# A decoder layer with 16384 single-neuron experts: 160 instead of 128 tokens by gathered rows, expert values as matmul weights, 1 MB weight transfers

## The chip, the cores and the metric

The kernel runs on one core of a Trainium2 chip. The core has a matmul engine (TensorE, PE in the profile; its weight loads are listed apart as PEld), three elementwise engines (VectorE = DVE, ScalarE = ACT, GpSimd = POOL), a queue engine (SyncE = SP) and 16 DMA engines between the chip's memory and the on-chip buffer. The metric is the device time of one execution in microseconds (us).

## The reference, cut to what matters

512 tokens of width 2048 pass through one layer: a projection, attention and a recurrent branch, an output projection, and then an expert network (PEER). Only its last part changes:

```python
def chunk(xc):                                   # xc: normalised tokens, (tokens, 2048)
    ...                                          # product keys: 8 heads x top 16 = 128 experts per token
    e = ...                                      # (tokens, 8, 16) expert numbers, of 16384
    g = jax.nn.softmax(top, axis=-1)
    ug = jnp.take(u_tab, e, axis=0)
    act = gelu(jnp.einsum('chkd,cd->chk', ug, xc))
    vg = jnp.take(v_tab, e, axis=0)
    return jnp.einsum('chk,chkd->cd', g * act, vg)
```

Each token picks 128 of 16384 rows of `u_tab` and of `v_tab` (each 16384 x 2048, float32). The result is added to the residual.

## The kernel before, in words

float32 products are made from three matmuls: each operand is split into a part `hi` that the matmul takes exactly and a rest `lo`, and hi·hi, hi·lo and lo·hi are summed (`mm3`, L160; L982 to L984). The splits of weights are L130 (ACT, `hi`) and L131 (DVE, `lo`).

Weights stream through one helper. `order` (L77 to L103) lists units of 128 x 1024 floats (512 KB) in the order of their use; `need` (L135) hands out the next one and calls `emit_next` (L117) for as long as a place is free: it loads a unit (SP's queue, tile `raw`) and splits it. Each pool has two `raw` and two pairs `hi`, `lo`; with an extra pool open there are four of each.

The expert network is done in two ways. The first 128 tokens are **gathered**: for each of a token's 128 experts POOL fetches one row per token, 1 MB at a time (`gather`, L803), and DVE does one operation of 128 x 2048 on it (`side`, L813): for the table u a dot product with the token (L821), for v a multiplication by its weight added to the sum in `acc` (L826). Two tiles take turns for rows. The other 384 tokens (TD) are **dense**: TensorE computes all 16384 experts, and a gate that is zero for all but a token's 128 experts is multiplied on.

- An S job is a block of 128 experts of u: 48 matmuls, `hi`, `lo` of u as weights and 384 tokens as the moving operand (L161 to L163, output `pS`); then Gelu (L959), gate (L904) and split (L913, L916) into `ph`, `pl`. Part of these lie in places of the tiles FH, FL that the gathered tokens no longer need.
- A V job is four blocks times 512 columns of v: 36 matmuls, `ph`, `pl` of 128 tokens as weights and `hi`, `lo` of v, 512 columns, as the moving operand (L982 to L984, output `pV`); DVE adds the three sums to `acc` (L996).

The stages of the expert network, in time: norm and transposition of the tokens (L626 to L640); queries and top-k (the tables' keys, DVE's MAX8 and so on); the gate stage, which makes the gate matrix (L839 to L868) and runs S jobs whose results are stored (`park`, L665; 44 in all); the mixed stage, in which S jobs of the other 84 blocks and V jobs take turns; the tail, V jobs of the 44 stored blocks. In the mixed stage and the tail (`tc.manual_schedule`, L890) every engine works in the order of the code; before, a scheduler sets it. `pace` (L921) calls `side` at a rate: 0.585 per half job, 0.43 in the tail, and some in the gate stage. `post` holds what is to be done with a job's sums; it is emitted in the first half of the next job.

## Time and profile before

| | |
|---|---|
| median of 3 runs | 3100.5 us (3100.32 to 3105.6) |
| the profiled execution: device time | 3107.04 us |
| its span in the profile | 3104.9 us |
| TensorE busy / VectorE busy | 98% / 74% of the span |
| memory traffic | 691 MB, 223 GB/s over the span |
| stages (us from the start) | projections 0 to 297, attention 297 to 580, output projection 580 to 673, norm 673 to 688, top-k 688 to 965, gate 965 to 1349, mixed 1349 to 2700, tail 2700 to 3100 |

A row of matmuls in the profile has a mean duration that is longer than the distance from one to the next, since they are pipelined; what one costs in a stream is read from the starts. In a group's row, what stands behind the bar is idle time of the engine before these instructions and who ended it.

### The profile page before, as it was taken

The page shows a single profiled execution, that of the slowest core. Times are in us where ns is not written, and L with a number is a line of the kernel's source. Part 1 is how long each engine was busy: PE and PEld are TensorE (multiplying, and loading weights), DVE is VectorE, ACT ScalarE, POOL GpSimd, SP SyncE. Part 2 cuts the span into 40 slices and gives each one's busy share as a digit, 9 for nine tenths or more (in the row PEclk, how much of TensorE's full clock was granted, in tenths as well). Part 3 has the DMA queues.
Part 4 walks back from the last instruction along what each step waited for, and adds up shares of the span by engine and source line. Part 5 has one row for each costly group of instructions (what it writes and reads, how often), then busy time and mean ns, then how long its engine had stood idle before and what let it go on. Part 6 is the DMA issues. An engine that isn't in the chain of part 4 may idle for free.

```text
span 3104.9 us, 39324 instructions
## 1 busy us (share of the span) xinstructions
PE 3043.2 (98%) x15443; PEld 2630.8 (85%) x15443; DVE 2284.7 (74%) x3456; ACT 1096.5 (35%) x1371; POOL 393.9 (13%) x280
## 2 busy tenths in 40 slices
PE   8999999999999999999999999999999999999999
PEld 7777565678899998999999999999999999888887
DVE  4465544448999888757777777777777777788887
ACT  4455332342234444443333333333333333333332
POOL 0000000000000011001212112122211212211111
PEclk9999898999999999999999999999999999999999
DMA  7222211232245887678787787877878778878876
GB/s 247 87 78 75 88 55 41 88 108 83 89 129 195 269 274 255 200 264 290 278 296 284 283 301 274 299 284 281 296 281 296 285 282 292 298 277 295 290 283 234
DMA packets 247306, 691.13 MB, mean 223 GB/s; under 512 B 17040, under 2 KB 128272, under 8 KB 213456
## 3 DMA queue, kind: packets, MB, share of 16 engines
q1 hardware_dynamic: 152832, 382.15, 36.8%
q0 software_dynamic: 37008, 269.50, 23.2%
q10 hardware_dynamic: 57280, 36.97, 3.9%
q8 instruction: 121, 1.98, 0.3%
q14 instruction: 65, 0.53, 0.0%
HBM read 650.40 MB, written 38.14 MB: 222 GB/s over the span
## 4 chain that ended last, share of the span: by engine, by line
PE 57%; issue 0%; DVE 0%; ACT 0%
PE pV L984 11%; PE pV L983 11%; PE pV L982 11%; PE pS L161 8%; PE pS L163 8%; PE pS L162 8%; PE ps L161 0%; PE ps L162 0%; PE ps L163 0%; PE ps L863 0%; DVE acc L996 0%; ACT pact L674 0%; DVE o L850 0%; ACT hi L130 0%
## 5 line engine op out<-in xcount | busy, mean ns | idle before, releaser
L130 ACT ACTIVATE hi<-raw 128x1024 fp32r<-128x1024 f32 x631 | 667.8, 1061 | 1489.4 <-PE pS L162 487.6
L131 DVE TENSOR_TENSOR lo<-raw,hi 128x1024 fp32r<-128x1024 f32 x631 | 771.1, 1222 | 495.2 <-ACT hi L130 481.6
L161 PE MATMUL pS<-FH,hi 128*128 128x384 f32 x1344 | 449.9, 335 | 1.3 <-ACT pact L674 1.3
L163 PE MATMUL pS<-FH,lo 128*128 128x384 f32 x1344 | 450.0, 335 | 0.0
L162 PE MATMUL pS<-FL,hi 128*128 128x384 f32 x1344 | 449.5, 334 | 0.0
L984 PE MATMUL pV<-hi,FL 128*128 128x512 f32 x960 | 374.7, 390 | 0.0
L983 PE MATMUL pV<-lo,FH 128*128 128x512 f32 x960 | 374.7, 390 | 0.0
L982 PE MATMUL pV<-hi,FH 128*128 128x512 f32 x960 | 373.4, 389 | 0.0
L161 PE MATMUL ps<-FH,hi 128*128 128x384 f32 (+1 forms) x960 | 342.8, 357 | 0.3 <-ACT hi L130 0.3
L809 POOL DMA_INDIRECT row<-in_un,E x128 | 175.6, 1372 | 1319.3 <-DVE row L821 819.3
L163 PE MATMUL ps<-FH,lo 128*128 128x384 f32 (+1 forms) x960 | 337.8, 352 | 0.6 <-DVE lo L131 0.6
L162 PE MATMUL ps<-FL,hi 128*128 128x384 f32 (+1 forms) x960 | 338.1, 352 | 0.0
L821 DVE SCALAR_TENSOR_TENSOR row<-row,xg 128x2048 f32<-128x2048 f32 x128 | 292.5, 2285 | 22.0 <-DMA row<-in_un,E 22.0
L826 DVE SCALAR_TENSOR_TENSOR acc<-row,W,acc 128x2048 f32<-128x2048 f32 x128 | 300.2, 2345 | 0.0
L809 POOL DMA_INDIRECT row<-in_vn,E x128 | 192.4, 1503 | 804.8 <-DVE acc L826 754.0
L161 PEld LDWEIGHTS pS<-FH,hi 128*128 128x128 f32 x1344 | 252.3, 188 | 4.7 <-ACT pact L674 1.7
L162 PEld LDWEIGHTS pS<-FL,hi 128*128 128x128 f32 x1344 | 252.3, 188 | 3.1
L163 PEld LDWEIGHTS pS<-FH,lo 128*128 128x128 f32 x1344 | 252.2, 188 | 0.0
L996 DVE TENSOR_TENSOR acc<-pV,acc 128x512 f32<-128x512 f32 x384 | 240.9, 682 | 8.3 <-PE pV L984 8.3
L984 PE MATMUL pV<-hi,pl 128*128 128x512 f32 x576 | 224.4, 390 | 0.0
L983 PE MATMUL pV<-lo,ph 128*128 128x512 f32 x576 | 224.2, 389 | 0.0
L982 PE MATMUL pV<-hi,ph 128*128 128x512 f32 x576 | 224.0, 389 | 0.0
(281 smaller groups left out, 4423.2 us busy)
## 6 DMA issues: line engine op xcount, KB each, us to landing
raw<-in_ud SPq DMA_DIRECT2D x256, 512.0 KB
raw<-in_vd SPq DMA_DIRECT2D x256, 512.0 KB
G<-GD SPq DMA_DIRECT2D x33, 768.0 KB
GD<-stg ACTq DMA_DIRECT2D x12, 2048.0 KB
raw<-in_win SPq DMA_DIRECT2D x44, 512.0 KB
raw<-in_wo SPq DMA_DIRECT2D x32, 512.0 KB
raw<-in_wq SPq DMA_DIRECT2D x32, 512.0 KB
AD<-pact ACTq DMA_DIRECT2D x44, 192.0 KB
```

The source lines that it names most:

```text
L130: s.activation(hi, raw, AF.Copy)
L131: v.tensor_tensor(lo, raw, hi.bitcast(F32), op=OP.subtract)
L161: pe.matmul(out, ah, bh, start=start, stop=False)
L162: pe.matmul(out, ah, bl, start=False, stop=False)
L163: pe.matmul(out, al, bh, start=False, stop=stop)
L809: g.indirect_dma_start(out=r, out_offset=None, in_=d["un" if j < 128 else "vn"], in_offset=bass.IndirectOffsetOnAxis(ap=E0[:, j % 128:j % ...
L821: v.scalar_tensor_tensor(r, r, 1.0, xg, op0=OP.mult, op1=OP.mult, accum_out=dots[:, j:j + 1])
L826: v.scalar_tensor_tensor(acc[:, 0, :], r, W0[:, j - 128:j - 127], acc[:, 0, :], op0=OP.mult, op1=OP.add)
L982: pe.matmul(pss[t], ph[:, t, :], hi[:, cs], start=pr + bj == 0, stop=False)
L983: pe.matmul(pss[t], ph[:, t, :], lo[:, cs], start=False, stop=False)
L984: pe.matmul(pss[t], pl[:, t, :], hi[:, cs], start=False, stop=pr + bj == 2)
L996: v.tensor_tensor(a, pss[t], a, op=OP.add)
```

## The change

The gathered tokens become 160: 128 as before (E0) and 32 more (EX). For these 32 the 128 experts are laid out as 4 groups of 32 partitions times 32 columns, so that 32 more gathers of 128 rows serve each table: 320 gathers in place of 256. Rows may live in five homes (a tile A, the place in `acc` of the first 128 tokens, whose residual waits in memory as RD, the tile X of the token operand, and from the mixed stage on Y and C); which row goes where is a list made at build time. The 32 tokens' sums over four groups are added by a matmul with a 0/1 matrix at the end. The dense tokens become TD = 352.

In a V job `hi`, `lo` of v are now the weights (128 columns each) and `ph`, `pl` of 352 tokens the moving operand: 48 matmuls of 352 columns, whose sums are transposed (features by tokens). So `acc` of the dense tokens is transposed once at the start (48 transposes into `hold`, then a copy by POOL into `acc`), and transposed back at the end (`write_out`). The sums of a V job are two tiles of two banks, each added in one DVE operation of 128 x 704. Of eight blocks' `ph`, five lie in FH, FL as 11 pieces of 32 columns, one as 4 pieces of 88, two in tiles of their own.

Weights are loaded 1 MB at a time (two units, 8 KB per partition): `bring` loads into a pool's one `raw` of 128 x 2048, `split` splits a half.

```diff
-TD = S - 128
+TX = 32
+XQ = 128 // TX
+EB = 2
+TG = 128 + TX
+TD = S - TG
...
+    def bring():
+
+        if moved[0] >= len(groups):
+            return False
+        keys, src = groups[moved[0]]
+        ps = pools if moved[1] + len(keys) <= limit[0] else pools[:1]
+        ps = [p for p in ps if not busy[id(p)]]
+        if not ps:
+            return False
+        p = ps[0]
+        moved[0] += 1
+        moved[1] += len(keys)
+        busy[id(p)] = True
+        raw = p.tile([128, 2048], F32, name="raw", bufs=1)[:, :len(keys) * 1024]
+        sy.dma_start(raw, src if len(keys) == 1 else src.rearrange("p u c -> p (u c)"))
+        raws.append([raw, p, len(keys), 0])
+        return True
+
+    def split():
...
         hi = p.tile([128, 1024], F32R, name="hi", bufs=2)
         lo = p.tile([128, 1024], F32R, name="lo", bufs=2)
         s.activation(hi, raw, AF.Copy)
         v.tensor_tensor(lo, raw, hi.bitcast(F32), op=OP.subtract)
...
+        if r[3] == r[2]:
+            raws.pop(0)
+            busy[id(r[1])] = False
         return True
...
-    XH = fbig.tile([128, NTT, KT, 128], F32R, name="FH")
-    XL = fbig.tile([128, NTT, KT, 128], F32R, name="FL")
-    ex = open_extra("ex2", None)
-    fp = pool("ffn")
+    XH = fbig.tile([128, KT, S], F32R, name="FH")
+    XL = fbig.tile([128, KT, S], F32R, name="FL")
+    fp = pool("ffn", side="right")
...
     v.tensor_tensor(xg, xns[0], grow, op=OP.mult)
+    v.tensor_tensor(grow[:TX], xns[1][:TX], grow[:TX], op=OP.mult)
+    sy.dma_start(XD, grow[:TX])
+    sy.dma_start(RD[0:128], acc[:, 0, :])
+    sy.dma_start(RD[128:128 + TX], acc[:TX, 1, :])
+
+    acc2 = acc.rearrange("p t c -> p (t c)")[:, D:D + KT * TD]
+    accT = acc2.rearrange("p (k n) -> p k n", n=TD)
+    hold = fp.tile([128, KT, TD], F32, name="hold")
+    for k in range(KT):
+        ps = bank()
+        for t in range(1, NTT):
+            pe.transpose(ps[:, t * 128:(t + 1) * 128], acc[:, t, k * 128:(k + 1) * 128], ident)
+        s.activation(hold[:, k, :], ps[:, TG:], AF.Copy)
+    g.tensor_copy(acc2, hold.rearrange("p k n -> p (k n)"))
     close(fp)
+    ex = open_extra("ex2", None)
...
+    SLOTS = [(tab, e, j) for tab in ("un", "vn") for e, n in ((E0, 128), (EX, NX)) for j in range(n)]
+    def gather():
+
+        while ng[0] < len(SLOTS):
+            i = ng[0]
+            p = place[i]
+            if not free[p] or p not in home:
+                return
...
+            g.indirect_dma_start(out=r, out_offset=None, in_=d[tab],
+                                 in_offset=bass.IndirectOffsetOnAxis(ap=e[:, j:j + 1], axis=0))
...
-        if q % 3 == 0:
+        if q % 8 in (0, 3, 6):
             park()
-            if q % 6 == 3 or q > 42:
-                side(rowp)
+        if q % 8 == 0 or q % 16 == 11:
+            side()
...
+    def write_out(dc):
+
+        for t0 in range(0, TD, 128):
+            n = min(128, TD - t0)
+            ps = wide()[:, 0]
+            for i in range(4):
+                pe.transpose(ps[:n, i * 128:(i + 1) * 128], accT[:, 4 * dc + i, t0:t0 + n], ident)
+            o = ep.tile([128, NCH, GRP, 32], F32, name="G", bufs=2).rearrange("p c a t -> p (c a t)")[:n, :512]
+            s.activation(o, ps[:n], AF.Copy)
+            s.dma_start(d["out"][TG + t0:TG + t0 + n, dc * 512:(dc + 1) * 512], o)
...
-    RATE = 0.585
+    RATE = 0.81
...
                 for k in range(8):
                     kk = hf * 8 + k
                     mm3(ps, hi[:, k * 128:(k + 1) * 128], lo[:, k * 128:(k + 1) * 128],
-                        XH[:, 1:, kk, :], XL[:, 1:, kk, :], kk == 0, kk == KT - 1)
+                        XH[:, kk, TG:], XL[:, kk, TG:], kk == 0, kk == KT - 1)
...
-                for t in range(3):
+                for i in range(4):
                     for bj in range(2):
                         ph, pl = Pt[gi * GRP + 2 * pr + bj]
-                        cs = slice(bj * 512, (bj + 1) * 512)
-                        pe.matmul(pss[t], ph[:, t, :], hi[:, cs], start=pr + bj == 0, stop=False)
-                        pe.matmul(pss[t], ph[:, t, :], lo[:, cs], start=False, stop=False)
-                        pe.matmul(pss[t], pl[:, t, :], hi[:, cs], start=False, stop=pr + bj == 2)
+                        ws = slice(bj * 512 + i * 128, bj * 512 + (i + 1) * 128)
+                        pe.matmul(pss[i], hi[:, ws], ph, start=pr + bj == 0, stop=False)
+                        pe.matmul(pss[i], lo[:, ws], ph, start=False, stop=False)
+                        pe.matmul(pss[i], hi[:, ws], pl, start=False, stop=pr + bj == 2)
...
-                pace(0.43 if tail else RATE)
+                pace(0.4 if tail else RATE)
...
+                for i, pw in enumerate(pws):
+                    a = accT[:, 4 * dc + EB * i:4 * dc + EB * (i + 1), :]
+                    v.tensor_tensor(a, pw[:, :, :TD], a, op=OP.add)
```

What it moves is seen in the order of each engine's instructions. First TensorE, from a V job to an S job in the mixed stage, before (pV and pS are sums, behind the arrow stand both operands, FH and FL here are blocks' `ph`, `pl` or the tokens; the last numbers are the output's partitions x columns):

```order
L982 MATMUL pV<-hi,FH 128x512
L983 MATMUL pV<-lo,FH 128x512
L984 MATMUL pV<-hi,FL 128x512
L161 MATMUL pS<-FH,hi 128x384
L162 MATMUL pS<-FL,hi 128x384
L163 MATMUL pS<-FH,lo 128x384
```

The same place now:

```order
L1129 MATMUL pw<-FH,hi 128x352
L1130 MATMUL pw<-FH,lo 128x352
L1131 MATMUL pw<-FL,hi 128x352
L191 MATMUL pw<-FH,hi 128x352
L192 MATMUL pw<-FL,hi 128x352
L193 MATMUL pw<-FH,lo 128x352
```

Both kinds of job are now 48 matmuls of 352 columns. Second ScalarE at the end of the norm stage, before (FH is the `hi` of the tokens, `hi<-raw` the split of weights, qT the first query's copy):

```order
L630 ACTIVATE xn_4165<-acc,r_4153 128x2048
L130 ACTIVATE hi<-raw 128x1024
L637 ACTIVATE FH<-ps,vec 128x4x128 x16
L130 ACTIVATE hi<-raw 128x1024 x3
L730 ACTIVATE qT<-ps 128x512
```

The same place now:

```order
L671 ACTIVATE xn_4097<-acc,r_4085 128x2048
L677 ACTIVATE FH<-ps,vec 128x512 x16
L693 ACTIVATE hold<-ps 128x352 x16
L152 ACTIVATE hi<-raw 128x1024 x2
L784 ACTIVATE qT<-ps 128x512
```

The 16 copies into `hold` stand before the next split of weights, and that split goes into tiles that lie where `hold` lay, so it also waits for POOL's copy out of `hold` (L694). Third SP's queue in the mixed stage, before (`raw` from u and v, G the gates of four blocks):

```order
L127 DMA raw<-in_ud 128x1024 x2
L127 DMA raw<-in_vd 128x1024
L895 DMA G<-GD 128x12x128
L127 DMA raw<-in_vd 128x1024
L127 DMA raw<-in_ud 128x1024 x2
```

The same place now:

```order
L135 DMA raw<-in_vd 128x2048
L135 DMA raw<-in_ud 128x2048
L1025 DMA G<-GD 128x11x128
L135 DMA raw<-in_vd 128x2048
L135 DMA raw<-in_ud 128x2048
```

Two loads of 512 KB have become one of 1 MB, of which two places exist in place of four of half the size.

## Rows read from the trace of the kernel before

**Rows 1.** The page: span, and busy time of TensorE and VectorE.

```profile
span 3104.9 us, 39324 instructions
PE 3043.2 (98%) x15443; PEld 2630.8 (85%) x15443; DVE 2284.7 (74%) x3456; ACT 1096.5 (35%) x1371; POOL 393.9 (13%) x280
```

**Rows 2.** Busy time by stretch: norm, top-k, gate, mixed, tail; columns in the first line.

```profile
core 0: us, PE busy (x) PEld busy (x) DVE busy (x) ACT busy (x) POOL busy (x), PEclk, DMA share, GB/s
...
688.00:965.00 277.00, 276.15 (x1401) 245.23 (x1402) 257.51 (x947) 88.72 (x117) 0.00 (x0) 1.00 0.34 108
965.00:1349.00 384.00, 359.49 (x2769) 351.17 (x2768) 299.84 (x600) 174.42 (x196) 31.81 (x26) 0.97 0.75 243
...
1700.00:2200.00 500.00, 500.00 (x2542) 456.64 (x2542) 386.52 (x400) 155.24 (x182) 101.87 (x71) 1.00 0.81 290
...
2700.00:3095.00 395.00, 395.00 (x1744) 327.06 (x1743) 338.62 (x371) 121.64 (x141) 66.27 (x41) 1.00 0.80 281
```

**Rows 3.** TensorE in order of time, three starts (us): V half job, S job, V job.

```profile
1893.08 0.39 PE L982 MATMUL pV<-hi,ph 128*128 128x512 f32 x1
...
1897.16 0.33 PE L161 MATMUL pS<-FH,hi 128*128 128x384 f32 x1
...
1905.50 0.39 PE L982 MATMUL pV<-hi,FH 128*128 128x512 f32 x1
```

**Rows 4.** TensorE in order of time: matmuls of 128 columns with own weights.

```profile
704.35 0.94 PE L691 MATMUL ps<-keys,qT 128*128 128x128 f32 x7
```

**Rows 5.** VectorE in order of time, mixed stage.

```profile
1895.51 2.29 DVE L821 SCALAR_TENSOR_TENSOR row<-row,xg 128x2048 f32<-128x2048 f32 x1
1897.72 0.08 DVE L821 DVE_READ_ACCUMULATOR row<-row,xg 128x1 f32 x1
1898.45 1.23 DVE L131 TENSOR_TENSOR lo<-raw,hi 128x1024 fp32r<-128x1024 f32 x1 [0.64 <-ACT hi L130]
1899.59 1.88 DVE L996 TENSOR_TENSOR acc<-pV,acc 128x512 f32<-128x512 f32 x3
...
1907.77 0.55 DVE L904 TENSOR_TENSOR pact<-pact,G 128x384 f32<-128x384 f32 x1
1908.91 0.56 DVE L916 TENSOR_TENSOR FL<-pact,FH 128x384 fp32r<-128x384 f32 x1 [0.59 <-ACT FH L913]
```

**Rows 6.** Groups of VectorE, 1700 to 2200 us: count, busy us, mean ns, idle before.

```profile
L131 DVE TENSOR_TENSOR lo<-raw,hi 128x1024 fp32r<-128x1024 f32 x121 | 148.0, 1223 | 92.6 <-ACT hi L130 92.6
```

**Rows 7.** DMA queues, 1700 to 2200 us: packets, MB, time of 16 engines; a gather's landing.

```profile
q1 hardware_dynamic: 29772, 69.46, 41.0%
q0 software_dynamic: 10290, 74.99, 39.2%
...
row<-in_un,E POOLq DMA_INDIRECT x54, 7.2
```

**Rows 8.** Two stretches of 10 us with the DMA engines full (columns as in Rows 2).

```profile
2040.00:2050.00 10.00, 10.00 (x51) 8.95 (x50) 7.63 (x10) 2.65 (x3) 2.29 (x2) 1.00 0.99 370
2580.00:2590.00 10.00, 10.00 (x51) 8.95 (x50) 6.41 (x6) 3.87 (x5) 0.94 (x1) 1.00 1.05 388
```

**Rows 9.** Groups by shape: weight split; POOL's sum; gate; ScalarE's copy; VectorE's scaling.

```profile
L130 ACT ACTIVATE hi<-raw 128x1024 fp32r<-128x1024 f32 x631 | 667.8, 1061 | 1489.4 <-PE pS L162 487.6 <-PE ps L162 402.1 <-PE pV L984 362.5
...
L332 POOL TENSOR_TENSOR xs<-xs,yg 128x512 f32<-128x512 f32 x4 | 5.2, 1298 | 81.7 <-ACT yg L331 81.5
...
L863 PE MATMUL ps<-o,o 128*128 128x128 bf16 x1152 | 75.8, 223 | 24.5 <-ACT stg L865 12.3 <-DVE o L850 11.4
L959 ACT ACTIVATE pact<-pS 128x384 f32<-128x384 f32 x84 | 39.7, 473 | 0.0
...
L628 DVE TENSOR_SCALAR xn<-acc,r 128x2048 f32<-128x2048 f32 x2 | 2.5, 1284 | 0.0
```

**Rows 10.** The end, in order of time; and landing of a 1 MB output (us).

```profile
3099.82 0.69 DVE L996 TENSOR_TENSOR acc<-pV,acc 128x512 f32<-128x512 f32 x1 [0.67 <-PE pV L984]
3100.55 0.38 ACTq L999 DMA_DIRECT2D out<-acc  x1
...
out<-acc POOLq DMA_DIRECT2D x1, 1024.0 KB, 4.4
```

**Rows 11.** Projections of 512 columns, moving operand in one piece (XH) and in four (FH).

```profile
L161 PE MATMUL ps<-XH,hi 128*128 128x512 f32 x352 | 142.2, 405 | 7.8 <-ACT hi L130 7.8
...
L161 PE MATMUL ps<-FH,hi 128*128 128x512 f32 x256 | 101.0, 395 | 0.0
```

More of the change, by code (lines that the diff above doesn't have):

```diff
@@ L154, in close_extra @@
         pools.remove(p)
-        assert all(r[2] is not p for r in ready.values())
+        assert all(r[2] is not p for r in ready.values()) and all(r[1] is not p for r in raws)
         if last[0] is p:
@@ L791, in body @@
         park()
+        if t == 1:
+            ei = tk.tile([128, 128], I32, name="ei")
+            v.scalar_tensor_tensor(ei[:TX], ef[0][:TX], 128.0, ef[1][:TX], op0=OP.mult, op1=OP.add)
+            sy.dma_start(ED, ei[:TX])
+            sy.dma_start(HD, gf[:TX])
+            for q in range(XQ):
+                rows_, cols_ = slice(q * TX, (q + 1) * TX), slice(q * 128 // XQ, (q + 1) * 128 // XQ)
+                sy.dma_start(EX[rows_], ED[:, cols_])
+                sy.dma_start(GX[rows_], HD[:, cols_])
         if t > 1:
@@ L801, in body @@
     rows, ng = {}, [0, 0]
-    def gather(*pools):
-        j = ng[0]
-        if j >= 256:
-            return
-        ng[0] += 1
-        r = pools[j % len(pools)].tile([128, D], F32, name="row", bufs=1)
-        g.indirect_dma_start(out=r, out_offset=None, in_=d["un" if j < 128 else "vn"],
-                             in_offset=bass.IndirectOffsetOnAxis(ap=E0[:, j % 128:j % 128 + 1], axis=0))
-        rows[j] = r
-    def side(*pools):
-        j = ng[1]
-        if j >= 256:
+    NX = 128 // XQ
@@ new lines, in body @@
+    SLOTS = [(tab, e, j) for tab in ("un", "vn") for e, n in ((E0, 128), (EX, NX)) for j in range(n)]
+    U1, V0, V1 = 128, 128 + NX, 256 + NX
+    NG0 = NCH + NCH // 2 + 1
+    home, used_at, place, late = {"A": rowp.tile([128, D], F32, name="rowA"), "B": acc[:, 0, :], "X": xg}, {}, [], {}
+    for i in range(len(SLOTS)):
+        if i < NG0:
+            c = "AB"
+        elif i < U1:
+            c = "ABCY" if i < U1 - 4 else "ABC"
+        elif i < V0:
+            c = "ABCX" if i < V0 - 4 else "ACX"
+        elif i < V1:
+            c = "ACXY" if i < V1 - 4 else "ACY"
+        else:
+            c = "ACY"
+        if i in (U1, V0):
+            used_at["X" if i == U1 else "Y"] = i + 0.5
+        p = min(c, key=lambda p: used_at.get(p, -1))
+        used_at[p] = i
+        place.append(p)
@@ new lines, in body @@
+    free = {p: True for p in "ABCXY"}
+    last_use = {p: {} for p in "ABCXY"}
+    ycut, bcut = max(i for i in range(U1) if place[i] == "Y"), max(i for i in range(V0) if place[i] == "B")
+    xcut = max(i for i in range(V1) if place[i] == "X")
+    def gather():
[4 more added lines that the diff above has]
+                return
+            ng[0] += 1
+            free[p] = False
+            tab, e, j = SLOTS[i]
+            r = home[p]
+            g.indirect_dma_start(out=r, out_offset=None, in_=d[tab],
+                                 in_offset=bass.IndirectOffsetOnAxis(ap=e[:, j:j + 1], axis=0))
+            rows[i] = r
@@ L829, in side @@
-        gather(*pools)
+        for p in freed:
+            free[p] = True
+        freed.clear()
+        r = rows.pop(i)
+        tab, e, j = SLOTS[i]
+        first, n = e is E0, 128 if e is E0 else NX
+        if tab == "un":
+            x_ = xg if first else home["Y"]
+            v.scalar_tensor_tensor(r, r, 1.0, x_, op0=OP.mult, op1=OP.mult, accum_out=dots[:, j:j + 1])
+            if j == n - 1:
+                w, g_ = (W0, G0) if first else (WX, GX)
+                s.activation(w, dots[:, :n], AF.Gelu)
+                v.tensor_tensor(w, w, g_, op=OP.mult)
+        elif first:
+            v.scalar_tensor_tensor(acc[:, 0, :], r, W0[:, j:j + 1], acc[:, 0, :], op0=OP.mult, op1=OP.add)
+            if j == n - 1:
+                g.dma_start(d["out"][0:128, :], acc[:, 0, :])
+        elif j == 0:
+            v.tensor_scalar(xg, r, WX[:, 0:1], None, op0=OP.mult)
+        else:
+            v.scalar_tensor_tensor(xg, r, WX[:, j:j + 1], xg, op0=OP.mult, op1=OP.add)
@@ L831, in body @@
+        freed.append(place[i])
+        if i == ycut:
+            freed.pop()
+            for q in range(XQ):
+                g.dma_start(home["Y"][q * TX:(q + 1) * TX], XD)
+        elif i == bcut:
+            freed.pop()
+            g.dma_start(acc[:, 0, :], RD[0:128])
+        elif i == xcut:
+            freed.pop()
+        if i == U1 - 1:
+            freed.append("X")
+        elif i == V0 - 1:
+            freed.append("Y")
+        gather()
     gp = pool("gate")
@@ L924, in pace @@
             debt[0] -= 1
-            side(rowp, ep)
-    gather(rowp, ep)
+            side()
+    gather()
     post = []
```

177 lines of the change are left out of this document (101 added, 76 removed).

## The prediction, made before the changed kernel ran

> **What bounds the kernel now.** I read the page's busy times first, then the same by stretch, then starts in order of time, since a matmul's duration in a group's row overlaps with its neighbours'. The page puts TensorE at 98% of the span and VectorE at 74% [rows 1]. By stretch [rows 2] TensorE is busy 500.00 of 500 us in the mixed stage, 395.00 of 395 in the tail and 276.15 of 277 in top-k; only the gate stage leaves it 24.5 us. The granted clock is 1.00 in the mixed stage and the tail, the upper of its two levels. So a matmul that becomes shorter shortens these stages, until something else does not keep up. The candidates stand in the same row of the mixed stage: VectorE 386.5 of 500, and the DMA engines at a share of 0.81, moving 290 GB/s.
>
> **What a matmul costs.** Between 1893.08 and 1897.16 lie 18 matmuls of 512 columns, so 226.7 ns each; between 1897.16 and 1905.50 lie 48 of 384 columns, 173.8 ns each [rows 3]. The difference is 0.413 ns a column, which leaves a fixed 15.0 ns, and 352 columns come to 160.5 ns. That is below anything shown with float32 operands of this kind, so I ask whether loading the weights becomes the bound: seven matmuls of 128 columns, each with weights of its own of the same size, took 0.94 us, at most 134 ns each [rows 4]. That is less than 160.5, so the line holds.
>
> **The terms, against the profiled execution's 3107.0 us** (it stands 6.5 us above the median of 3100.5; the sum is a difference, and I take it off the median).
>
> S jobs: 48 matmuls, 8.34 us before, 7.70 now, 128 of them: −81 us. V jobs: 36 × 226.7 ns = 8.16 us before, 48 × 160.5 = 7.70 now, 128 of them: −59. There are more matmuls than before and yet it is less, since 4 × 352 columns replace 3 × 512; the twelve extra fixed costs are in the 160.5. Gate matrix: 88 steps in place of 96; a step's matmuls keep TensorE busy 75.8/96 = 0.79 us [rows 9]: −6. Together −146.
>
> Norm stage: 48 transposes at up to 0.134 us are 6.4 us, and the 16 copies into `hold` at 0.47 us (L959's, of 384 columns) 7.6, of which TensorE, eight banks ahead, sees about 6. What stands behind them is a chain: POOL's copy of 128 x 5632, then the split of the next query weights (1.06 and 1.22 us) [rows 6, 9]. TensorE has one load, 48 × 227 ns = 10.9 us, in hand meanwhile. POOL's copy is not in the trace. At the pace of its sum of two operands, 1298 ns for 512, it takes 14.3 us, and TensorE waits about 9; at that of VectorE's scaling of one operand, 1284 ns for 2048, 3.5 us, and the chain is hidden. I take a copy of 7 us and a wait of 2, half of the nearest row on POOL itself, since one operand is read in place of two. The term is +8, bounds 6 and 15. The Trainium skill (GPSIMD Engine Reference, section Engine selection) says that operations with one input run on GpSimd roughly at VectorE's line rate; by that the wait of 2 us goes. No run so far shows it.
>
> End: the last sum was added at 3099.82, the span ended 5.1 us later [rows 10]. Now the last two column groups leave by six copies through two tiles, so three rounds of a copy (0.5 us) and a write, at most the 4.4 us of a 1 MB write [rows 10], and the 32 tokens' sum runs beside that: 9 to 15 us in place of 5, I take +6. Transposing back the two column groups before it puts 24 transposes into the tail and makes TensorE wait for VectorE's addition a job early: +6. Together +12, bounds 8 and 18.
>
> Loads of 1 MB: in projections and top-k an extra pool is open and 10.9 us of matmuls cover a load. In the attention stage only one place is left, and a unit can be loaded only when the one before it has been split: half of the gather's 7.2 us for 1 MB [rows 7] plus 2.3 us of split is 5.9 us against 24 × 227 ns = 5.4 us of matmuls, for ten units: +5 with nothing between them, 0 if attention's own matmuls lie between, and below 0 nothing, as TensorE was not waiting for loads there. I take +3.
>
> Mixed stage, 80 pairs of an S and a V job, 16.5 us each before and 15.4 by TensorE alone. The cost of 64 more gathers lies here, since `pace` now asks for 0.81 per half job: 3.24 rows a pair in place of 2.34. VectorE, by distances between starts [rows 5]: four `lo` at 1.14, the sums 1.88, gate and split 1.70 with the wait for ScalarE, 2.34 rows at 2.21: 13.3 us of 16.5. Now two additions of 704 columns at 0.80 (0.60 for 512, and 1.05 ns a column from `lo` against it), so 4.56 + 1.60 + 1.70 + 7.16 = 15.0 us of 15.4. It was idle 92.6 us in 500 waiting for `hi` [rows 6], that is, ahead of TensorE; this cushion goes. Behind a late VectorE wait the sums: before, they were added by 1901.47, 4.3 us after the V job's end [rows 5], and a bank came round again two V jobs later; now the second tile is needed when the next V job starts, 7.7 us on.
>
> DMA: a pair moved 2 × 1.05 + 2.34 × 1.05 + 0.2 MB (gates) = 4.75 MB in 16.5 us, the 290 GB/s of rows 2. Now it is 2.10 + 3.40 + 0.18 = 5.68 MB in 15.4 us, 369 GB/s. The engines' time per MB is 16 × 500 × 0.410/69.46 = 47 us on q1 (pieces of 4 KB) and 42 us on q0 (8 KB) [rows 7]; with weights in pieces of 8 KB too, 5.68 MB take 238 us of 16 engines, 14.9 us of 15.4. So three resources are at 97% and over. What speaks for holding 369 is that whole stretches of 10 us ran at 370 and 388 [rows 8], and that a row has four homes, so some 15 us from issue to use in place of 12. Bounds: 0, if TensorE stays at 500 of 500; and at the far end the 290 GB/s of now, 19.6 us a pair, +336. I take the rate nearest to rows 8, a little under 370: 360 GB/s, 15.75 us a pair, 80 × 0.35 = +28. The Trainium skill (DMA: Bandwidth & Descriptors, section Specifications) gives about 358 GB/s as the memory's limit for one core; by it a pair takes 15.9 us and the term is +37. Both stretches of rows 8 are above that limit, so the trace does not agree with it for short times.
>
> Tail: a V job moves 1.05 + 0.84 + 0.36 MB in 7.7 us, 292 GB/s against 281 [rows 2], and VectorE has 0.8 rows in place of 0.86: nothing changes there. GpSimd's more gathers and the EX lists cost nothing as long as VectorE is what they wait for.
>
> Sum: −146 + 8 + 12 + 3 + 28 = −95, so 3012 by the profiled execution and 3006 by the median.
>
> **Rivals.** (1) TensorE stays the only bound: +0 in the mixed stage, +0 for loads and the low ends elsewhere: −146 + 14 = −132, 2968 us. For it: 500 of 500 now. Against: the three shares above. (2) The mixed stage goes over to DMA or VectorE: 16.2 to 16.9 us a pair (351 to 336 GB/s), +64 to +120, 3042 to 3098. For it: the share of 0.81 at 290 GB/s, scaled to 369, is 1.03. Against: larger pieces cost less, and rows 8. (3) Slower: the DMA engines cannot hold 335 GB/s over the whole stage. Everything but the mixed stage is worth −123, or 1.54 us a pair; 5.68 MB in 16.9 us are 335 GB/s, and below that the change loses. At 320 GB/s a pair takes 17.75 us, 3166 us in all. For it: no stretch of 500 us has shown more than 290. Against: those were not asked for more, since TensorE never waited. (4) Moving operands in 11 pieces of 32 columns, five of eight blocks, 3840 matmuls: if a piece had a price of 2.2 ns, 25 ns a matmul, it would eat the gain of 95; at the fixed 15 ns each it would be +580. Against: 512 columns in one piece and in four have means of 405 and 395 ns [rows 11], so a piece costs nothing that shows.
>
> **Chances.** Forecast (2985 to 3030) 0.55; rival 1 0.20; rival 2 0.17; rival 3 0.05; rival 4 0.03. The range of 8 in 10 goes from just under rival 1 to the middle of rival 2: 2960 to 3065. A measurement of this kernel can tell about 0.2%, 6 us, from no change. Faster by more than that: 0.90; within it 0.03; slower 0.07.
>
> **What would show it.** S and V jobs both at 7.7 us apart in the tail, matmuls 160 ns apart: rival 4 is out. In the mixed stage TensorE's idle time and who ended it: VectorE's `lo` or sums (late VectorE), or `hi` behind a load (late DMA); GB/s of the stretch near 360. A wait of TensorE for `hi` just after the first query weights shows POOL's copy, whose row then has its duration. Wrong would be: TensorE idle in the tail, top-k longer by more than 15 us, or matmuls of 352 columns no faster than those of 384.

## The result, and the profile after

The changed kernel takes 3029.9 us (median of 4 runs, 3025.2 to 3040.8); the kernel before, on the same chip, 3103.05 (3100.3 to 3113.5). The ratio is 0.9763, 95% interval 0.9727 to 0.9799: 73 us faster. The forecast was 3006 with a range of 2960 to 3065. The profiled execution took 3028.0 us, its span is 3026.0 us. The page (busy time of each engine, share, instructions), against [rows 1]:

```profile
span 3026.0 us, 41804 instructions
...
PE 2932.1 (97%) x16987; PEld 2692.1 (89%) x16987; DVE 2370.1 (78%) x3391; ACT 1082.9 (36%) x1392; POOL 576.2 (19%) x350
```

Busy time by stretch, for top-k, gate, mixed stage and tail, against [rows 2]:

```profile
core 0: us, PE busy (x) PEld busy (x) DVE busy (x) ACT busy (x) POOL busy (x), PEclk, DMA share, GB/s
699.00:990.00 291.00, 281.71 (x1436) 248.79 (x1435) 262.27 (x955) 90.16 (x120) 11.23 (x5) 0.98 0.34 122
990.00:1356.00 366.00, 328.21 (x2640) 319.00 (x2639) 260.27 (x531) 162.99 (x185) 16.32 (x13) 0.95 0.64 212
1700.00:2200.00 500.00, 499.21 (x3088) 498.91 (x3087) 461.41 (x439) 161.43 (x195) 176.08 (x109) 1.00 0.96 369
2625.00:3010.00 385.00, 381.39 (x2345) 380.24 (x2344) 324.80 (x324) 122.06 (x145) 62.14 (x39) 1.00 0.77 281
```

In the mixed stage TensorE is as busy as before, while VectorE went from 386.5 to 461.4 of 500 us, and the DMA engines from a share of 0.81 and 290 GB/s to 0.96 and 369. In the gate stage TensorE is idle for 38 of 366 us and its granted clock is 0.95: that stretch became worse.

Where the time went, by the first matmul of each stage, the tail from the end of the last S job (the forecast's terms are put on stages by the number of jobs: 11, 33 and 84 S jobs in top-k, gate and mixed stage; 80 and 48 V jobs in mixed stage and tail):

| stage | before | after | difference | forecast |
|---|---|---|---|---|
| projections | 297.4 | 305.9 | +8.5 | 0 |
| attention, output projection | 380.2 | 374.5 | -5.7 | +3 |
| norm to first query weights | 10.2 | 18.5 | +8.3 | +8 |
| top-k | 282.8 | 291.2 | +8.5 | -7 |
| gate | 380.2 | 366.5 | -13.7 | -27 |
| mixed | 1349.1 | 1266.3 | -82.7 | -63 |
| tail | 399.9 | 390.4 | -9.5 | -16 |
| after the last V matmul | 5.2 | 12.6 | +7.4 | +6 |
| span | 3104.9 | 3026.0 | -78.9 | -95 |

A V job, an S job and the next V job in the mixed stage, TensorE in order of time, against [rows 3]:

```profile
1891.75 0.32 PE L1129 MATMUL pw<-FH,hi 128*128 128x352 f32 x1
...
1899.64 0.32 PE L191 MATMUL pw<-FH,hi 128*128 128x352 f32 x1
...
1907.31 0.32 PE L1129 MATMUL pw<-FH,hi 128*128 128x352 f32 x1
```

The S job takes 7.67 us, 159.8 ns a matmul; the V job 7.89 us, 164.4 ns. VectorE's groups (count, busy, mean ns, idle before) and the DMA engines in 1700 to 2200 us, against [rows 6, 7]:

```profile
L153 DVE TENSOR_TENSOR lo<-raw,hi 128x1024 fp32r<-128x1024 f32 x129 | 157.0, 1221 | 18.8 <-ACT hi L152 18.7
L1143 DVE TENSOR_TENSOR acc<-pw,acc 128x704 f32<-128x704 f32 x66 | 55.5, 882 | 0.0
```

```profile
DMA packets 35953, 184.52 MB, mean 369 GB/s; under 512 B 2895, under 2 KB 14159, under 8 KB 14159
## 3 DMA queue, kind: packets, MB, share of 16 engines
q0 software_dynamic: 15309, 111.15, 56.4%
q1 hardware_dynamic: 20610, 72.89, 38.8%
```

VectorE's cushion, the time it waits for `hi`, fell from 92.6 to 18.8 us, as forecast, but nothing came through it to TensorE. The gate matrix, against the row of L863 in [rows 9], where 24.5 us of idle time stood:

```profile
L989 PE MATMUL ps<-o,o 128*128 128x128 bf16 x1056 | 73.4, 224 | 42.2 <-DVE o L976 40.7
```

The longest of these waits, ScalarE, VectorE and TensorE in order of time:

```profile
1024.74 0.38 ACTq L994 DMA_DIRECT2D GD<-stg  x1
...
1046.74 2.73 ACT L991 ACTIVATE stg<-ps 128x512 f32<-128x512 f32 x3 [14.86 <-DMA GD<-stg]
1049.28 1.99 ACT L152 ACTIVATE hi<-raw 128x1024 fp32r<-128x1024 f32 x2
1050.36 1.23 DVE L153 TENSOR_TENSOR lo<-raw,hi 128x1024 fp32r<-128x1024 f32 x1 [10.78 <-ACT hi L152]
...
1054.52 0.29 PE L989 MATMUL ps<-o,o 128*128 128x128 bf16 x1 [12.97 <-DVE o L976]
```

Read from the bottom: TensorE waits 13 us for one-hot products, VectorE is late with them since it stood 10.8 us before a `lo`, whose `hi` stands on ScalarE behind a copy into `stg`; and `stg`, of which there is one, was still being written to memory, 22 us after that write was issued.

The norm stage (VectorE and GpSimd in order of time):

```profile
682.61 2.29 DVE L680 TENSOR_TENSOR xg<-xn,grow 128x2048 f32<-128x2048 f32 x1 [1.76 <-DMA grow<-in_fg]
684.94 2.28 DVE L681 TENSOR_TENSOR grow<-xn,grow 32x2048 f32<-32x2048 f32 x1
687.15 10.61 DVE L678 SCALAR_TENSOR_TENSOR FL<-ps,vec,FH 128x512 fp32r<-128x512 f32 x16
...
700.18 4.89 POOL L694 COPY acc<-hold 128x5632 f32<-128x5632 f32 x1 [108.71 <-ACT hold L693]
...
706.24 2.35 DVE L153 TENSOR_TENSOR lo<-raw,hi 128x1024 fp32r<-128x1024 f32 x2
```

The start (SyncE's loads, then TensorE) and the end (VectorE, ScalarE, SyncE), in order of time:

```profile
1.68 0.42 SPq L135 DMA_DIRECT2D raw<-in_win  x1
...
2.62 0.43 SPq L230 DMA_DIRECT2D cst<-in_cst  x1
7.12 0.33 SPq L221 DMA_DIRECT2D xs<-in_xT  x1
7.49 2.85 SPq L135 DMA_DIRECT2D raw<-in_win  x2
...
19.81 0.79 PE L191 MATMUL ps<-XH,hi 128*128 128x512 f32 x1 [2.85 <-ACT XH L225]
...
3013.50 0.89 DVE L1143 TENSOR_TENSOR acc<-pw,acc 128x704 f32<-128x704 f32 x1 [1.03 <-PE pw L1131]
3016.67 0.59 ACT L1077 ACTIVATE G<-pw 96x512 f32<-96x512 f32 x1 [1.07 <-DMA out<-G]
...
3022.02 0.34 SPq L1163 DMA_DIRECT2D out<-rowA  x1
```

### The profile page after: what moved, and what is told of

Its sections match the earlier page's. It is cut to its first block, busy times and chain, and to the rows that moved or that the text cites. A ratio compares the mean times of both kernels' runs of the same rounds, so it can differ in the third digit from the quotient of the medians.

```text
span 3026.0 us, 41804 instructions
## 1 busy us (share of the span) xinstructions
PE 2932.1 (97%) x16987; PEld 2692.1 (89%) x16987; DVE 2370.1 (78%) x3391; ACT 1082.9 (36%) x1392; POOL 576.2 (19%) x350
## 4 chain that ended last, share of the span: by engine, by line
PE 67%; DVE 10%; issue 8%; DMA 8%; POOL 4%; ACT 3%; ACTq 0%; POOLq 0%; SPq 0%; DVEq 0%
PE pw L1129 8%; PE pw L1131 8%; PE pw L1130 7%; PE ps L191 6%; PE ps L193 6%; PE ps L192 6%; PE pw L191 5%; PE pw L193 4%; PE pw L192 4%; DMA GD<-stg 3%; DVE lo L153 3%; PE ps L421 2%; PE ps L422 2%; PE ps L423 2%; DVE acc L934 2%
## 5 line engine op out<-in xcount | busy, mean ns | idle before, releaser
L1129 PE MATMUL pw<-FH,hi 128*128 128x352 f32 x1536 | 502.0, 327 | 4.5 <-DVE acc L1143 3.3
L1131 PE MATMUL pw<-FL,hi 128*128 128x352 f32 x1536 | 501.9, 327 | 0.0
L1130 PE MATMUL pw<-FH,lo 128*128 128x352 f32 x1536 | 500.0, 326 | 0.0
L191 PE MATMUL pw<-FH,hi 128*128 128x352 f32 x1344 | 434.3, 323 | 0.6 <-ACT pact L728 0.6
L193 PE MATMUL pw<-FH,lo 128*128 128x352 f32 x1344 | 433.9, 323 | 0.0
L192 PE MATMUL pw<-FL,hi 128*128 128x352 f32 x1344 | 433.2, 322 | 0.0
L193 PE MATMUL ps<-FH,lo 128*128 128x352 f32 (+1 forms) x960 | 332.1, 346 | 4.9 <-DVE lo L153 4.9
L191 PE MATMUL ps<-FH,hi 128*128 128x352 f32 (+1 forms) x960 | 336.6, 351 | 0.0
L192 PE MATMUL ps<-FL,hi 128*128 128x352 f32 (+1 forms) x960 | 331.8, 346 | 0.0
L1129 PEld LDWEIGHTS pw<-FH,hi 128*128 128x128 f32 x1536 | 288.8, 188 | 6.0 <-issue 4.1
L1131 PEld LDWEIGHTS pw<-FL,hi 128*128 128x128 f32 x1536 | 288.9, 188 | 0.0
L1130 PEld LDWEIGHTS pw<-FH,lo 128*128 128x128 f32 x1536 | 288.7, 188 | 0.0
L191 PEld LDWEIGHTS pw<-FH,hi 128*128 128x128 f32 x1344 | 252.9, 188 | 0.9 <-ACT pact L728 0.9
L192 PEld LDWEIGHTS pw<-FL,hi 128*128 128x128 f32 x1344 | 253.4, 189 | 0.0
L193 PEld LDWEIGHTS pw<-FH,lo 128*128 128x128 f32 x1344 | 252.4, 188 | 0.0
L1143 DVE TENSOR_TENSOR acc<-pw,acc 128x704 f32<-128x704 f32 x256 | 215.5, 883 | 8.4 <-PE pw L1131 8.3
L191 PEld LDWEIGHTS ps<-FH,hi 128*128 128x128 f32 x960 | 184.4, 192 | 14.4 <-issue 4.4
## 6 DMA issues: line engine op xcount, KB each, us to landing
GD<-stg ACTq DMA_DIRECT2D x11, 2048.0 KB, 12.2
```

The lines of the kernel that those rows point to most:

```text
L191: pe.matmul(out, ah, bh, start=start, stop=False)
L192: pe.matmul(out, ah, bl, start=False, stop=False)
L193: pe.matmul(out, al, bh, start=False, stop=stop)
L1129: pe.matmul(pss[i], hi[:, ws], ph, start=pr + bj == 0, stop=False)
L1130: pe.matmul(pss[i], lo[:, ws], ph, start=False, stop=False)
L1131: pe.matmul(pss[i], hi[:, ws], pl, start=False, stop=pr + bj == 2)
```

## The experiments

e1 to e8 and e11 are edits of the changed kernel, e9 is one of e8, e10 and e12 of e9. The kernel before had medians of 3105 to 3110 us beside them, so runs are compared by their ratio to it; the changed kernel's is 0.9763 (0.9727 to 0.9799).

| run | median us | ratio to before, 95% | norm starts | top-k | gate | mixed | tail | end |
|---|---|---|---|---|---|---|---|---|
| changed kernel | 3029.9 | 0.9763 | 680.5 | 291.2 | 366.5 | 1266.3 | 390.4 | 12.6 |
| e1 gate rows | 3007.9 | 0.9670 (0.9654, 0.9686) | 682.9 | 289.1 | 345.5 | 1281.9 | 391.8 | 12.5 |
| e2 start | 3034.1 | 0.9747 (0.9726, 0.9769) | 679.7 | 290.8 | 373.2 | 1269.2 | 389.9 | 12.5 |
| e3 pieces | 3021.8 | 0.9727 (0.9705, 0.9750) | 679.9 | 287.8 | 367.5 | 1264.4 | 389.8 | 12.6 |
| e4 extra load | 3108.6 | 0.9991 (0.9979, 1.0004) | 680.8 | 288.9 | 372.5 | 1337.3 | 401.1 | 12.5 |
| e5 other place | 3017.0 | 0.9716 (0.9690, 0.9741) | 669.3 | 287.5 | 363.3 | 1266.7 | 389.5 | 12.6 |
| e6 roles alone | 3186.2 | 1.0259 (1.0233, 1.0285) | 675.2 | 285.8 | 390.1 | 1379.5 | 421.3 | 14.0 |
| e7 half MB | 3026.5 | 0.9740 (0.9718, 0.9763) | 671.5 | 288.3 | 360.3 | 1280.9 | 386.7 | 12.2 |
| e8 together | 3008.0 | 0.9681 (0.9658, 0.9703) | 674.0 | 287.6 | 348.9 | 1274.9 | 397.9 | 9.8 |
| e9 sum last | 2997.3 | 0.9650 (0.9635, 0.9665) | 673.7 | 290.0 | 346.8 | 1264.5 | 390.1 | 11.8 |
| e10 rows slower | 3007.7 | 0.9679 (0.9666, 0.9693) | 671.7 | 287.9 | 348.0 | 1263.5 | 404.6 | 11.8 |
| e11 one bank | 3029.2 | 0.9751 (0.9736, 0.9766) | 677.4 | 287.9 | 372.3 | 1265.6 | 391.9 | 12.1 |
| e12 rows later | 3004.5 | 0.9669 (0.9652, 0.9686) | 673.5 | 291.4 | 340.7 | 1272.5 | 387.7 | 11.8 |

The stages are those of each profiled execution. The mixed stage of one kernel can differ by some 15 us between executions (e1's profiled one, at 3024.1, is its slowest of five). Stages that an edit did not touch differ too: top-k takes 287.5 to 291.2 us in the eleven kernels whose top-k is that of the changed kernel, the gate stage 360.3 to 373.2 in the seven that have its gate stage and its tokens. One execution cannot tell smaller differences than these.

**The roles alone** (e6): the 32 tokens are dense again.

```diff
-TG = 128 + TX
+TG = 128
...
-    RATE = 0.81
+    RATE = 0.59
...
```

> The 32 extra tokens are dense again: 384 dense tokens, 256 gathers in four homes (A, B, C, X) at 0.59 per half job, all else as in the changed kernel (values as weights, sums two banks at a time, 1 MB loads). Theory A (the gain is the 32 tokens' alone, and changing the roles of the V matmuls by itself costs): S jobs 8.34 us as before, V jobs 48 x about 175 ns = 8.4 us against 8.16 before, +31 us; norm stage +8, end +6, projections +8: 3145-3165 with the kernel before at 3105. Rival B (the roles, the larger sums or the 1 MB loads bring a share of the 73 us themselves): 3060-3105.

Measured: 3186 us, slower than before by 2.6%. Theory A holds, with a larger price than its 3145 to 3165. An S job, a V job and the next S job:

```profile
1893.45 0.34 PE L191 MATMUL pw<-FH,hi 128*128 128x384 f32 x1
...
1901.89 0.34 PE L1098 MATMUL pw<-FH,hi 128*128 128x384 f32 x1
...
1910.29 0.34 PE L191 MATMUL pw<-FH,hi 128*128 128x384 f32 x1
```

The S job takes 8.44 us (8.34 before), the V job 8.40 and on average 48 x 176.8 ns = 8.49, against 8.16 in the old arrangement. So the new roles lose 0.3 us a job; they are what lets 32 tokens fewer shorten the V matmul at all, and these 32 are worth about 155 us (1.0259 - 0.9763 of 3105).

**The gate stage** (e1).

```diff
-    GD = dr.tile([NCH, NBLK // GRP, 128, GRP * 32], F32, name="GD")
+    GD = dr.tile([NCH, 128, NBLK // GRP, GRP * 32], F32, name="GD")
...
-            s.dma_start(GD[q // 8].rearrange("g p x -> p g x"), stg[0].rearrange("p (g a) t -> p g (a t)", a=GRP))
+            s.dma_start(GD[q // 8], stg[0].rearrange("p (g a) t -> p g (a t)", a=GRP))
...
```

> The stored gate matrix GD is laid out so that a partition's 16 KB are written in one piece (before: 32 pieces of 512 B); nothing else changes. Theory A (the gate stage lost its gain because ScalarE waits in order for the 2 MB write of stg, with the weight splits queued behind it): ScalarE's wait for GD, 68.1 us in the gate stage, falls below 30, TensorE's and its loads' wait for the one-hot products, 58.9 us, falls below 25, the gate stage goes from 366.5 to 330-345 us, the run to 2998-3010. Rival B (VectorE works the gathered rows in order between the one-hots, and that is what delays them): the GD wait falls, TensorE's wait stays above 45, the run stays at 3024-3036. Rival C (the write is slow from the traffic beside it, not from its pieces): the write still lands after 11 us or more and nothing changes.

Measured: 3007.9 us, gate stage 345.5, just above the 330 to 345 of theory A. ScalarE's wait for GD fell from 68.1 to 36.6 us, less than expected; the first write is free after 13.6 us instead of 22.0. TensorE's row, and ScalarE's wait (us in total, times, longest):

```profile
L989 PE MATMUL ps<-o,o 128*128 128x128 bf16 x1056 | 71.7, 224 | 23.4 <-DVE o L976 22.5
```

```profile
ACT stg L991 <- DMA GD<-stg: 36.6, 10, 6.6
```

Theory A holds: the order of rows on VectorE was not touched, and TensorE's idle time went from 42.2 to 23.4 us, about the 24.5 of the kernel before.

**The start** (e2, e5).

```diff
-        if m == 0:
+        if m < 2:
...
```

> The weights of the second input block, like those of the first, are loaded as two transfers of 512 KB; all else 1 MB as in the changed kernel. Theory A (projections lost 8.5 us because 1 MB of later weights goes ahead of the token loads that TensorE needs): TensorE's waits for XH and hi behind the first matmul, 5.9 us, fall below 2, attention starts at 298-301 us instead of 305.9, the run is 4-8 us faster than the changed kernel. Rival B (the 1 MB loads cost time through the whole stage, by the single place per pool): attention starts at 304-306, the run changes by less than 2 us.

Measured: attention starts at 305.1, and the wait of 2.85 us for XH is still there at 19.85. Theory A falls in this form. SyncE's rows after show why: the second `raw` is issued at 7.49, since its place is that of the first, which has to be split before. The choice of place was next:

```diff
-        p = ps[0]
+        p = min(ps, key=lambda p: when.get(id(p), 0))
+        when[id(p)] = moved[0] + 1
...
```

> A load goes to the pool whose place was used longest ago, instead of to the first that is free (in the changed kernel the second half of the first input block waits for the place of the first half to be split and is issued at 7.49 us, beside the third token load, instead of at 2.60). Theory A (the 1 MB place costs the start, since two loads in a row use one place and token loads stand behind them): TensorE's waits for XH and XL in the first 36 us, 4.7 us, go below 1.5, attention starts at 297.5-301 us instead of 305.9, the run is 5-8 us faster than the changed kernel. Rival B (the 8.5 us come from the clock or from traffic that stays): attention starts at 304-306, change below 2 us.

Measured: attention starts at 297.4, as before the change, the waits for XH and XL are 0.7 us, and the run is 3017.0. Theory A holds for the waits. For the whole run its gain is not shown: the interval of its ratio overlaps that of the changed kernel. The second load now leaves at once (SyncE in order of time):

```profile
1.68 0.42 SPq L136 DMA_DIRECT2D raw<-in_win  x1
2.14 0.43 SPq L223 DMA_DIRECT2D xs<-in_xT  x1
2.62 0.43 SPq L136 DMA_DIRECT2D raw<-in_win  x1
```

Not all of the 8.5 us is the place, though. Four later kernels with this choice (e8, e9, e10, e12) start attention at 299.4 to 301.8 us, the changed kernel and the other runs that load 1 MB into the first free place at 301.7 to 308.5. TensorE's granted clock differs with it: in the first 36 us it was 1.00 before the change, in e5 and in e10, 0.95 in e8, e9 and e12, and 0.91 in the changed kernel. So the choice of place takes the waits away each time, and of the 8.5 us 4.1 to 6.5 came back in the later kernels.

**The pieces of the moving operand** (e3).

```diff
-        if q < 5:
-            ph, pl = XH[:, 0:NCH, 32 * q:32 * q + 32], XL[:, 0:NCH, 32 * q:32 * q + 32]
+        if q < 4:
+            av = a.rearrange("p (c t) -> p c t", c=4)
+            ph, pl = (X[:, 4 * q:4 * q + 4, 0:TD // 4] for X in (XH, XL))
...
```

> Of eight blocks' ph, pl, four lie in 4 pieces of 88 columns and two in 8 pieces of 44 (changed kernel: five in 11 pieces of 32, one in 4); two in tiles of their own as before. In the changed kernel matmuls with 11 pieces start 164.3 ns apart on average, with 4 pieces 161.3, with one 160.3. Theory A (a piece costs about 0.4 ns): those with 8 pieces come to about 163, the mean over V jobs from 163.1 to about 161.5, mixed stage and tail together 8-11 us shorter. Rival B (the place, not the pieces: operands in FH, FL are slower than in tiles of their own): all in FH, FL stay at 163-165, change below 3 us.

An S job, a V job (all operands in 4 pieces) and the next S job:

```profile
1895.54 0.32 PE L191 MATMUL pw<-FH,hi 128*128 128x352 f32 x1
...
1903.26 0.33 PE L1130 MATMUL pw<-FH,hi 128*128 128x352 f32 x1
...
1910.95 0.32 PE L191 MATMUL pw<-FH,hi 128*128 128x352 f32 x1
```

The V job takes 7.69 us, 160.2 ns a matmul, in FH and FL all the same: rival B falls. But theory A's price per piece is wrong too: operands in 8 pieces have a median distance of 163 to 164 ns, like those in 11; those in 4 have 160, like one. Mixed stage and tail of the profiled executions differ by only 2.5 us, because TensorE waited 9.3 us in V jobs there instead of 4.5. The medians differ by 8 us, but the intervals of the two ratios overlap: the shorter distance between matmuls is shown, a gain of the whole run is not.

**The limit of the DMA engines** (e4).

```diff
+    def extra():
+        sy.dma_start(XT[nx[0] % 2], d["un"][128 * (nx[0] % 100):128 * (nx[0] % 100) + 128, 0:256])
+        nx[0] += 1
...
+                extra()
...
+                if not tail:
+                    extra()
...
```

> In each half job of the mixed stage 128 KB more are loaded (pieces of 1 KB) into a tile that nothing reads: 403 GB/s would be asked for instead of 369. Theory A (DMA still has room above 369, TensorE alone bounds the stage): mixed stage 1266 us plus at most 10, run 3025-3040. Rival B (369 to 385 GB/s is what the DMA engines can do, the stage stands right at their limit): at 385 GB/s a pair takes 16.1 us instead of 15.4, mixed stage +40 to +60; at 370 GB/s 16.8 us, +110; TensorE then waits for hi and lo. Run 3070-3140.

Measured: 3108.6 us, mixed stage +71, as rival B said. Two stretches of it:

```profile
1700.00:2200.00 500.00, 474.19 (x2876) 468.22 (x2875) 431.61 (x419) 144.96 (x182) 159.60 (x103) 0.99 0.98 376
2200.00:2690.00 490.00, 476.07 (x2924) 473.51 (x2923) 439.93 (x343) 147.13 (x183) 182.22 (x99) 1.00 1.00 386
```

403 GB/s were asked for and 376 to 386 given, at a share of 0.98 to 1.00. So 9% more traffic turns the whole gain into nothing; the 369 of the changed kernel lie 2 to 4% below the limit of this mix of pieces.

The wait did not come to TensorE the way rival B said, by `hi` and `lo`. TensorE waited 51 us in the mixed stage, most of it for VectorE's sums (us in total, times, longest; then SyncE's wait before the extra loads):

```profile
PE pw L1136 <- DVE acc L1152: 34.5, 25, 2.2
SPq L1065 <- DMA xt<-in_un: 454.5, 174, 12.5
```

VectorE was late with the sums behind its own waits for `hi`, 120.7 us instead of 47.7 in the changed kernel. The second line is a rival that stays: an extra load waits in SyncE's queue until one of its two tiles has landed, and the weights' loads stand behind it. How much of the 71 us is this order, and how much the full DMA engines, was not separated; that the engines were full is shown by their share.

**512 KB loads** (e7).

```diff
-        raw = p.tile([128, 2048], F32, name="raw", bufs=1)[:, :len(keys) * 1024]
+        raw = p.tile([128, 1024], F32, name="raw", bufs=2)
...
```

> The weights come in transfers of 512 KB again (pieces of 4 KB, two places per pool of half the size); all else as in the changed kernel. Theory A (the mixed stage stands at the limit of the DMA engines and the 8 KB pieces keep it below): at 47 us of engine time per MB instead of 42 a pair needs 10 us more of 16 engines, 0.66 us of 15.4; the stage becomes 10-50 us longer, projections 6-8 us shorter; run 3030-3070. Rival B (the size of the pieces is nothing, the shorter transfers come sooner): mixed stage within 5 us, projections 6-8 us shorter; run 3017-3025.

Measured: 3026.5 us; by the ratios no difference that can be told. The mixed stage is 14.6 us longer, as theory A says, and the gain at the start is larger than either theory had. The mixed stage (1700 to 2200 us), and its queue of weights:

```profile
1700.00:2200.00 500.00, 488.61 (x3008) 487.23 (x3007) 453.57 (x428) 156.04 (x190) 172.29 (x107) 0.99 0.96 363
```

```profile
q1 hardware_dynamic: 29580, 71.98, 40.6%
```

A MB on q1 took 45.1 us of engine time instead of 42.6, and TensorE was idle for 11 us of 500 instead of 1. Since the mixed stage varies that much with 1 MB loads too (1281.9 us in e1), the tie between the two is likely and not shown.

**One bank at a time** (e11).

```diff
-EB = 2
+EB = 1
```

> The changed kernel with the sums of a V job added one bank at a time: four additions of 128 x 352 instead of two of 704, eight tiles of one bank. Theory A (the additions are covered either way): VectorE spends at most 0.3 us more per V job, TensorE waits no more than now, run 3022-3036. Rival B (VectorE, at 92% in the mixed stage, is so near its limit that the additions decide): 128 times 0.3 us show, run 3045-3070.

Measured: 3029.2 us. Theory A holds: VectorE 464.3 of 500 us instead of 461.4, TensorE 500.0. Adding two banks at a time was worth nothing that shows.

**Together** (e8, e9, e10): e1, e3 and e5 in one kernel, and six places for the last six copies. In e8 the 32 tokens' sum is also taken in the tail:

```diff
+                if ng[1] >= len(SLOTS) and not summed:
+                    sum_out()
...
```

> Four edits together: GD laid out so that a partition is written in one piece; ph, pl in 4 and 8 pieces; loads to the place used longest ago; at the end the 32 tokens' sum is taken as soon as the last row is done and the last six copies go to six places of the rows' tiles. Theory A (the gains add): gate -21, V matmuls -9, projections -6, end -5 against the changed kernel: 2985-2993. Rival B (the mixed stage stands at the DMA limit, so what the matmuls gain there comes back as waits): 2993-3003, with TensorE idle 8 us or more in the mixed stage.

Measured: 3008.0, above both ranges. TensorE waited 12.0 us in the mixed stage, as rival B said, and the tail was 7.5 us longer, which neither theory had. TensorE there:

```profile
2975.34 1.88 PE L1081 MATMUL pw<-xg,cst 128*32 128x512 f32 x4 [2.60 <-DVE xg L942]
2978.98 1.90 PE L1081 MATMUL pw<-xg,cst 128*32 128x512 f32 x4 [1.76 <-DVE rowA L1082]
```

> As the run with four edits together, but the 32 tokens' sum is taken at the very end again, as in the changed kernel (the last six copies keep their six places). Theory A (taken in the tail, that sum puts eight matmuls and two waits of 4.4 us into TensorE's stream, 7.5 us, and saves 2.8 at the end): tail 390 instead of 397.9, end 9.5-11, run 3000-3005. Rival B (the tail was longer from traffic): tail stays above 395, run 3006-3012.

Measured: 2997.3 us, ratio 0.9650, faster than the changed kernel beyond both intervals and the lowest ratio of all. Its interval overlaps those of e1, e8 and e12, so that the other edits add to e1's gain is likely and not shown. Theory A holds for the tail (390.1); the end, 11.8 us, gained less than expected. Against the changed kernel's profile: 6.8 us at the start, 19.7 in the gate stage, 4 in all the rest. The next edit is one of this kernel (e10):

```diff
-    RATE = 0.81
+    RATE = 0.77
...
-                pace(0.4 if tail else RATE)
+                pace(0.56 if tail else RATE)
```

> As the run beside it, with 0.77 instead of 0.81 rows per half job in the mixed stage and 0.56 instead of 0.40 in the tail: 352 to 358 GB/s are asked for in the mixed stage instead of 369, 318 to 322 instead of 280 in the tail. Theory A (the mixed stage stands so near the limit of the DMA engines that single late loads make TensorE wait): its waits in the mixed stage fall from 11 us to below 3, the run is 5-10 us faster than the one beside it and spreads less. Rival B (the waits come from VectorE's sums, with no tie to traffic): the run changes by less than 3 us, or VectorE, now at 93% in the tail, makes it 3-10 us slower there.

Measured: 3007.7 us. Rival B holds: the mixed stage gained 1 us, the tail lost 14.5. The 11 us of waits that theory A wanted to remove lay only by half in the mixed stage (5.5 us, now 3.8). TensorE's waits for VectorE's sums from 1357 us on, and the tail:

```profile
PE pw L1136 <- DVE acc L1150: 13.0, 18, 1.6
```

```profile
2620.00:2990.00 370.00, 355.90 (x2163) 347.11 (x2163) 327.26 (x314) 111.43 (x136) 78.36 (x47) 1.00 0.81 298
```

VectorE, busy for 327 of 370 us there, is late for the sums, and no row is among what it waits for from 2590 us on: it, not the traffic, sets how many rows the tail can take.

**Top-k** (e12, an edit of e9).

```diff
-            v.scalar_tensor_tensor(E0, ef[0], 128.0, ef[1], op0=OP.mult, op1=OP.add)
+            v.scalar_tensor_tensor(E0f, ef[0], 128.0, ef[1], op0=OP.mult, op1=OP.add)
...
+        if t == NTT - 1:
+            v.scalar_tensor_tensor(E0, ef[0], 0.0, E0f, op0=OP.mult, op1=OP.add)
```

> As the run with the sum taken last, but the expert numbers E0 that the gathers read are written after the last block of tokens' top-k instead of after the first, so that the scheduler cannot put a gathered row's operation (2.28 us of VectorE) into the middle of top-k. In the changed kernel two stand there (949 and 983 us), in the run with the sum taken last one at 941. Theory A (VectorE bounds the end of top-k, so such a row delays the gate stage by its own time): top-k 285-288 us instead of 290.0, the gate stage, where VectorE has time, unchanged within 3, run 2991-2996. Rival B (the 8.5 us come from TensorE's clock, 0.91 to 0.94 there, which has other causes): top-k 289-291, run within 2 us.

Measured: 3004.5 us, top-k 291.4. It does not tell the theories apart. The row's operation at 941 us left the middle of top-k, but e9 has a second one before the gate stage, which the expectation overlooked, and in e12 one stands at that place too and waits for its row (e9, then e12):

```profile
975.60 2.29 DVE L930 SCALAR_TENSOR_TENSOR acc<-acc,xg 128x2048 f32<-128x2048 f32 x1
977.92 2.29 DVE L933 SCALAR_TENSOR_TENSOR acc<-acc,xg 128x2048 f32<-128x2048 f32 x1 [7.44 <-DMA acc<-in_un,E]
```

Beside this, the two theories' ranges of top-k, 285 to 288 and 289 to 291 us, are no further apart than executions of the same top-k.

## Why the prediction was right, and where its steps were not

- **S jobs** (160.5 ns a matmul): right, 159.8.
- **V jobs** (160.5 ns): the term of -59 was too good by 15. Without TensorE's waits the mean distance is 163.0 ns: 164.5 in jobs with all operands in 11 pieces, 161.4 in the others; 2.5 ns x 48 x 128. Rival 4 was set aside because four pieces cost nothing [rows 11]; that row says nothing on eleven. e3 shows that the pieces do it. The term spreads over mixed stage and tail.
- **Mixed stage, DMA** (+28): this step failed. It took 360 GB/s (5.68 MB are 15.78 us by that, not 15.75, which would make the term +30); the engines carried the 369 that were asked for, and TensorE waited less than 2 us in the whole stage. Rival 1 was right for this stage; by e4, rival 2 began 2 to 4% above. The Trainium skill (DMA: Bandwidth & Descriptors, section Specifications) has about 358 GB/s as the limit of memory for one core, half of what it gives for a stack with two. The trace of this program, which runs on one core, does not agree: 369 over the stage and 386 in e4.
- **VectorE** (15.0 of 15.4 us a pair): near, 461.4 of 500 is 14.4 of the 15.6 us of rows 1891.75 to 1907.31; it stayed ahead.
- **Norm stage** (+8): right in sum, by other parts. GpSimd's copy took 4.89 us instead of 7 and TensorE did not wait; in its place VectorE came to FL 2.5 us later than before, since a second multiplication of 2.3 us and a wait of 1.8 us for the load of `grow` stood in front of it where a split of weights of 1.2 us had stood, and the 64 transposes took 12.7 us instead of 10.2. The Trainium skill (GPSIMD Engine Reference, section Engine selection) says that one-input operations run on GpSimd roughly at line rate; by that the wait goes, and it did. The trace agrees only roughly: GpSimd's copy took 0.87 ns an element of a partition, VectorE's scaling of one operand 0.63, GpSimd's sum of two 2.54 [rows 9].
- **Gate and S jobs in the gate stage** (-27): half came. They were counted at TensorE's full rate in the one stage where TensorE already waited 24.5 us [rows 2, 9]; its shorter work met the 2 MB write of `stg`, and the wait grew to 42.2 us. ScalarE had waited 61.7 us for that write before; now it was 68.1, the longest time 14.9 instead of 11.0. e1 shows the cause.
- **Top-k** (-7, came as +8.5): TensorE waited 9.5 us for VectorE, and in the last 90 us the granted clock was 0.94 and 0.91, a mean over stretches at the upper and, right behind the waits, at the lower of its two levels (before: 1.00). That two rows' operations stand there was not foreseen; whether they are the cause stays open after e12. This execution's 291.2 us are also the longest of the eleven with that top-k; the others lost 4.7 to 8.0 us.
- **1 MB loads** (0 in the projections, +3 in attention): it failed in the projections. I asked whether matmuls cover a load, not whether a place is free at the start. What it cost were waits, TensorE busy 21.3 us of the first 36 instead of 27.1, and the clock of 0.91 behind them; e5 takes the waits away. Attention and output projection became 5.7 us shorter, for a reason that was not followed up. With loads of 512 KB (e7) they took 377.6 us and with 1 MB in no run over 374.5, so a part may go with the size of the loads.
- **End** (+6) and **tail** (+6 for the last outputs): +7.4; the tail differs from the forecast by 6.5 us, what 48 V jobs lose by their pieces (48 x 48 x 2.5 ns = 5.8).

Of what the prediction named as signs that it is wrong, none came: TensorE is not idle in the tail, top-k is 8.5 us longer, and matmuls of 352 columns are faster. The misses largely cancel: +15 for pieces, +8.5 at the start, about +14 in the gate stage and +15 in top-k stand against -28 for a wait that did not come and -9 in attention. That the span shrank by 79 us where 95 were forecast, nearer than most of these steps, is in part luck; what holds without it are the shorter S and V jobs and a mixed stage that kept up.
